# RMSNorm with relu: 4 MB contiguous chunks in place on one hardware DMA queue, and one vector instruction for scale and relu of 8 rows

## The chip, the cores and the metric

The kernel runs on one core of one Trainium2 chip. A time is the device time in microseconds of one execution; "before" is the median of 10 runs. The profile is of one execution. Its span is the time from the first to the last recorded instruction of the core; the execution's own time is a little longer.

## The reference

The input x is f32 of 16 x 1024 x 512, that is 16384 rows of 512 elements (33.55 MB), and the output has the same shape and type. gamma has 512 elements, eps is 1e-5.

```python
rms = np.sqrt(np.mean(x ** 2, axis=-1, keepdims=True) + eps)
x_norm = x / rms * gamma
return np.maximum(x_norm, 0).astype(np.float32)
```

Each row needs the sum of its squares, then every element is multiplied by gamma and by the row's reciprocal root, and is cut at zero. Every byte of x is read once from DRAM and every byte of the output is written once.

## The kernel before

The 128 partitions each own 128 consecutive rows. The loop runs over 16 tiles of K = 8 rows per partition (128 x 4096 elements, 2 MB). Within DRAM a tile is 128 pieces of 16 KB, one per partition, 256 KB apart.

For each tile:

- L62: SP's queue loads `x_tile`. The pool has four buffers of each kind of tile, so at most four loads run ahead; a load into a used buffer waits until ScalarE and VectorE have read the old contents.
- L70: VectorE multiplies x by gamma for all 8 rows in one `tensor_mul` and writes another tile, `xg`. `gammaK` is gamma in SBUF, repeated 8 times by a step of 0 over the rows.
- L74: ScalarE squares each row in one activation, with the row's sum as accumulator output (eight activations, each followed by an accumulator read). The squares themselves go to a scratch tile in SBUF.
- L77: ScalarE takes the root of the 8 means plus eps; L80: VectorE takes the reciprocal, `rstd`.
- L84: VectorE multiplies each row of `xg` by its `rstd` and takes the maximum with 0, one `tensor_scalar` per row, eight per tile. The result `o_tile` is bf16.
- L90: GpSimd's software queue stores `o_tile` and casts it to f32 on the way.

gamma itself is loaded first, by one transfer on SP's queue that reads it 128 times (L48, 256 KB). The loop is written in this order; the order of instructions within an engine is settled by a scheduler at build time (on VectorE the product of a later tile stands between the reciprocal and the scaling of some tiles). Loads and stores are on two queues, which share the 16 DMA engines.

Of the kernel before, what the change touches and what calls it, by code (L numbers as in the profile page):

```python
# [1 line left out]

# [4 lines left out]


@with_exitstack
def kernel(  # L10
    ctx: ExitStack,
    tc: tile.TileContext,
    x: bass.AP,
    gamma: bass.AP,
    eps: bass.AP,
    out: bass.AP,
):
    nc = tc.nc
    P = nc.NUM_PARTITIONS

    x2 = x.flatten_outer_dims()
    out2 = out.flatten_outer_dims()
    n, d = x2.shape
    assert n % P == 0
    rows_per_part = n // P
    inv_d = 1.0 / d

    xv = x2.rearrange("(p r) d -> p r d", p=P)
    ov = out2.rearrange("(p r) d -> p r d", p=P)

    K = 8
    nchunks = rows_per_part // K
    assert rows_per_part % K == 0

    BF = mybir.dt.bfloat16
    F32 = mybir.dt.float32

    singles = ctx.enter_context(tc.tile_pool(name="singles", bufs=1))
    pool = ctx.enter_context(tc.tile_pool(name="pool", bufs=4))
    small = ctx.enter_context(tc.tile_pool(name="small", bufs=4))  # L40

    gamma_sbuf = singles.tile([P, d], F32)
    gamma_bcast = bass.AP(
        tensor=gamma.tensor,
        offset=gamma.offset,
        ap=[[0, P], gamma.ap[0]],
    )
    nc.sync.dma_start(out=gamma_sbuf, in_=gamma_bcast)  # L48

    eps_sbuf = singles.tile([P, 1], F32)  # L50
    nc.vector.memset(eps_sbuf, eps)  # L51

    sq_scratch = singles.tile([P, d], F32)

    gammaK = bass.AP(tensor=gamma_sbuf.tensor, offset=gamma_sbuf[:].offset,
                     ap=[gamma_sbuf[:].ap[0], [0, K], gamma_sbuf[:].ap[1]])

    for i in range(nchunks):
        s = i * K

        x_tile = pool.tile([P, K, d], F32)
        nc.sync.dma_start(out=x_tile, in_=xv[:, s:s + K, :])  # L62

        rstd = small.tile([P, K], F32)
        rms = small.tile([P, K], F32)
        ss = small.tile([P, K], F32)
        xg = pool.tile([P, K, d], F32)
        o_tile = pool.tile([P, K, d], BF)

        nc.vector.tensor_mul(out=xg, in0=x_tile, in1=gammaK)  # L70

        for j in range(K):
            ssj = ss[:, j:j + 1]
            nc.scalar.activation(out=sq_scratch, in_=x_tile[:, j, :],  # L74
                                 func=mybir.ActivationFunctionType.Square,
                                 accum_out=ssj)
        nc.scalar.activation(out=rms, in_=ss,  # L77
                             func=mybir.ActivationFunctionType.Sqrt,
                             bias=eps_sbuf, scale=inv_d)
        nc.vector.reciprocal(out=rstd, in_=rms)  # L80

        for j in range(K):
            rj = rstd[:, j:j + 1]
            nc.vector.tensor_scalar(  # L84
                out=o_tile[:, j, :], in0=xg[:, j, :],
                scalar1=rj, scalar2=0.0,
                op0=mybir.AluOpType.mult, op1=mybir.AluOpType.max,
            )

        nc.gpsimd.dma_start(out=ov[:, s:s + K, :], in_=o_tile)  # L90


# [1 line left out]
_INS = ['x', 'gamma', 'eps']  # L94
_OUTS = [((16, 1024, 512), 'float32')]
#: Inputs that are plain numbers.
_NUMBERS = {'eps': 9.999999747378752e-06}


# [26 lines left out]
```

## Time and profile before

| | |
|---|---|
| median of 10 runs | 165.72 us (165.56 to 165.77) |
| the profiled execution's own time | 165.56 us |
| its span | 163.8 us |
| VectorE (DVE) busy | 122.8 us, 75% of the span |
| ScalarE (ACT) busy | 99.4 us, 61% |
| GpSimd (POOL) busy | 8.9 us, 5% |
| moved by DMA | 67.40 MB, mean 411 GB/s |

Busy time is an instruction's recorded time on its engine. A row of digits is the span in 40 slices, each digit the busy share in tenths. A line of a group gives the source line, engine, operation, output and inputs with partitions x elements and type, the count, then the busy time in us and the mean of one in ns, then the idle time of the engine just before it and what ended most of it. A timeline line gives start and duration in us, engine, line and operation; the bracket gives the idle time before it and what released it. A line of windows gives the window, its length, the busy time of VectorE, ScalarE and GpSimd in it with the number of instructions, the granted TensorE clock, the mean busy share of the DMA engines and the GB/s that they moved. SPq and POOLq are the instruction queues of SP and GpSimd, which issue transfers.

### The profile page before, as it was taken

The page shows a single profiled execution, that of the slowest core. Times are in us where ns is not written, and L with a number is a line of the kernel's source. Part 1 is how long each engine was busy: PE and PEld are TensorE (multiplying, and loading weights), DVE is VectorE, ACT ScalarE, POOL GpSimd, SP SyncE. Part 2 cuts the span into 40 slices and gives each one's busy share as a digit, 9 for nine tenths or more (in the row PEclk, how much of TensorE's full clock was granted, in tenths as well). Part 3 has the DMA queues.
Part 4 walks back from the last instruction along what each step waited for, and adds up shares of the span by engine and source line. Part 5 has one row for each costly group of instructions (what it writes and reads, how often), then busy time and mean ns, then how long its engine had stood idle before and what let it go on. Part 6 is the DMA issues. An engine that isn't in the chain of part 4 may idle for free.

```text
span 163.8 us, 565 instructions
## 1 busy us (share of the span) xinstructions
DVE 122.8 (75%) x161; ACT 99.4 (61%) x274; POOL 8.9 (5%) x20
## 2 busy tenths in 40 slices
DVE  0049979999999999969497794959959497099500
ACT  3049999999993928659193773919559193094000
POOL 0000010001010101010101001010000101001100
DMA  4999999999999999999999999999999999999994
GB/s 118 391 440 428 424 436 384 434 428 424 428 428 424 430 432 420 432 436 416 432 436 416 434 428 416 440 424 428 428 428 440 416 428 440 416 440 380 428 412 192
DMA packets 4755, 67.40 MB, mean 411 GB/s; under 512 B 528, under 2 KB 528, under 8 KB 656
## 3 DMA queue, kind: packets, MB, share of 16 engines
q1 hardware_dynamic: 2448, 33.82, 57.1%
q0 software_dynamic: 2304, 33.56, 49.4%
q14 instruction: 3, 0.02, 0.0%
HBM read 33.82 MB, written 33.55 MB: 411 GB/s over the span
## 4 chain that ended last, share of the span: by engine, by line
issue 50%; DVE 27%; ACT 8%; DMA 6%; POOL 3%; POOLq 0%; SPq 0%
DVE xg L70 15%; DVE o_tile L84 12%; ACT sq_scratch L74 7%; DMA x_tile<-in_x_dram 6%; POOL out_dram L90 3%; ACT L77 1%; DVE rstd L80 1%; ACT rms L77 0%; POOLq L121 0%; SPq L48 0%; POOLq L90 0%
## 5 line engine op out<-in xcount | busy, mean ns | idle before, releaser
L74 ACT ACTIVATE sq_scratch<-x_tile 128x512 f32<-128x512 f32 x128 | 80.6, 629 | 48.6 <-DMA x_tile<-in_x_dram 45.1
L70 DVE TENSOR_TENSOR xg<-x_tile,gamma_sbuf 128x4096 f32<-128x4096 f32 x16 | 70.5, 4407 | 29.1 <-DMA x_tile<-in_x_dram 29.1
L84 DVE TENSOR_SCALAR o_tile<-xg,rstd 128x512 bf16<-128x512 f32 x128 | 52.1, 481 | 0.1
L74 ACT ACTIVATION_READ_ACCUMULATOR sq_scratch<-x_tile 128x1 f32 x128 | 23.9, 186 | 0.0
L90 POOL DMA_DIRECT2D out_dram<-o_tile x16 | 8.7, 541 | 145.7 <-DVE rstd L80 119.6
L77 ACT ACTIVATE rms<-ss,eps_sbuf 128x8 f32<-128x8 f32 x16 | 4.8, 301 | 0.5
L80 DVE RECIPROCAL rstd<-rms 128x8 f32<-128x8 f32 x16 | 3.2, 197 | 1.2 <-ACT rms L77 1.2
L74 ACT ACT_TABLE_LOAD x1 | 1.3, 1283 | 0.7 <-PEq L107 0.7
L77 ACT ACT_TABLE_LOAD x1 | 1.3, 1283 | 0.0
L51 DVE MEMSET eps_sbuf<- 128x1 f32 x1 | 0.1, 59 | 0.8 <-PEq L107 0.8
L107 POOL MEMSET const-float32-0.0<- 128x1 f32 x1 | 0.1, 99 | 0.2 <-issue 0.2
L107 POOL MEMSET const-bfloat16-1.0<- 128x1 bf16 x1 | 0.1, 102 | 0.0
L107 POOL MEMSET const-uint8-127<- 128x1 uint8 x1 | 0.1, 100 | 0.0
L107 POOL MEMSET const-float32-1.0<- 128x1 f32 x1 | 0.1, 99 | 0.0
## 6 DMA issues: line engine op xcount, KB each, us to landing
x_tile<-in_x_dram SPq DMA_DIRECT2D x16, 2048.0 KB, 26.2
out_dram<-o_tile POOLq DMA_DIRECT2D x16, 2048.0 KB, 21.8
gamma_sbuf<-in_gamma_dram SPq DMA_DIRECT2D x1, 256.0 KB, 4.8
```

The lines of the kernel that those rows point to most:

```text
L51: nc.vector.memset(eps_sbuf, eps)
L70: nc.vector.tensor_mul(out=xg, in0=x_tile, in1=gammaK)
L74: nc.scalar.activation(out=sq_scratch, in_=x_tile[:, j, :], func=mybir.ActivationFunctionType.Square, accum_out=ssj)
L77: nc.scalar.activation(out=rms, in_=ss, func=mybir.ActivationFunctionType.Sqrt, bias=eps_sbuf, scale=inv_d)
L80: nc.vector.reciprocal(out=rstd, in_=rms)
L84: nc.vector.tensor_scalar(out=o_tile[:, j, :], in0=xg[:, j, :], scalar1=rj, scalar2=0.0, op0=mybir.AluOpType.mult, op1=mybir.AluOpType.max,)
L90: nc.gpsimd.dma_start(out=ov[:, s:s + K, :], in_=o_tile)
L107: nc = _bacc.Bacc("TRN2", target_bir_lowering=False, num_devices=1)
```

## The change

The rows are cut differently: chunk c of 8 is 2048 consecutive rows, 16 per partition (4 MB), and is one contiguous region of DRAM. There are six slots of 128 x 8192 f32; a chunk is loaded into its slot, worked on in place and stored from it. The output stays f32, so the store casts nothing and goes on SP's queue too. The order of all instructions is now that of the program text: six loads, then S0, S1, L6, S2, L7, S3 to S7 on SP's queue (S and L for the store and the load of a chunk). Within a chunk the work is done in two groups of 8 rows: eight squares (the squares go to a PSUM tile), the root, the gamma product in place, the reciprocal, and one `scalar_tensor_tensor` that takes the maximum with 0 and multiplies by `rstd`, whose access pattern repeats each row's value 512 times with a step of 0. Since `rstd` is positive, maximum and product may change places. gamma is loaded as four rows of 2 KB on ScalarE's queue (into partitions 0, 32, 64 and 96 of a cleared tile) and spread to all partitions by a shuffle on VectorE.

```diff
+    xv = x2.rearrange("(c p k) d -> c p k d", p=P, k=16)
+    ov = out2.rearrange("(c p k) d -> c p k d", p=P, k=16)
-    xv = x2.rearrange("(p r) d -> p r d", p=P)
-    ov = out2.rearrange("(p r) d -> p r d", p=P)
-    K = 8
-    nchunks = rows_per_part // K
+    K = 16
+    G = 8
+    nchunks = rows // K
+    nslots = 6
+    ngroups = K // G
...
+    ctx.enter_context(tc.manual_schedule())
-    nc.sync.dma_start(out=gamma_sbuf, in_=gamma_bcast)
...
+    def load(i):
+        nc.sync.dma_start(out=slot[i % nslots], in_=xv[i])
+    def store(i):
+        nc.sync.dma_start(out=ov[i], in_=slot[i % nslots])
...
+    def compute(i):
+        xt = slot[i % nslots]
+        for g in range(ngroups):
+            a, b = g * G, (g + 1) * G
+            for j in range(a, b):
+                nc.scalar.activation(out=junk, in_=xt[:, j, :], func=ACTF.Square,
+                                     accum_out=ss[i][:, j:j + 1])
+            nc.scalar.activation(out=rms[i][:, a:b], in_=ss[i][:, a:b],
+                                 func=ACTF.Sqrt, bias=eps_sb, scale=inv_d)
+            nc.vector.tensor_mul(out=xt[:, a:b, :], in0=xt[:, a:b, :], in1=gammaG())
+            nc.vector.reciprocal(out=rstd[i][:, a:b], in_=rms[i][:, a:b])
+            r = rstd[i][:, a:b]
+            rb = bass.AP(tensor=r.tensor, offset=r.offset,
+                         ap=[r.ap[0], r.ap[1], [0, d]])
+            nc.vector.scalar_tensor_tensor(
+                out=xt[:, a:b, :], in0=xt[:, a:b, :], scalar=0.0, in1=rb,
+                op0=ALU.max, op1=ALU.mult)
+    nc.vector.memset(gseed, 0.0)
+    nc.vector.memset(eps_sb, eps)
+    for q in range(0, P, 32):
+        nc.scalar.dma_start(out=gseed[q:q + 1, :], in_=gamma[None, :])
+    for i in range(min(nslots, nchunks)):
+        load(i)
+    nc.vector.stream_shuffle(gamma_sb, gseed, [0] * 32)
+    for i in range(min(nslots, nchunks)):
+        compute(i)
+    nxt = nslots
     for i in range(nchunks):
-        x_tile = pool.tile([P, K, d], F32)
-        nc.sync.dma_start(out=x_tile, in_=xv[:, s:s + K, :])
...
-        nc.vector.tensor_mul(out=xg, in0=x_tile, in1=gammaK)
...
-            nc.vector.tensor_scalar(
-                out=o_tile[:, j, :], in0=xg[:, j, :],
-                scalar1=rj, scalar2=0.0,
-                op0=mybir.AluOpType.mult, op1=mybir.AluOpType.max,
-            )
-        nc.gpsimd.dma_start(out=ov[:, s:s + K, :], in_=o_tile)
+        store(i)
+        if i >= 1 and nxt < nchunks:
+            load(nxt)
+            compute(nxt)
+            nxt += 1
```

In the changed kernel's own numbering L59 is the load, L62 the store, L74 the square, L76 the root, L78 the gamma product, L79 the reciprocal, L83 scale and relu, and L94 the shuffle.

More of the change, by code (lines that the diff above doesn't have):

```diff
@@ L6 @@
 from concourse._compat import with_exitstack
+F32 = mybir.dt.float32
+ALU = mybir.AluOpType
+ACTF = mybir.ActivationFunctionType
 @with_exitstack
@@ L23 @@
     n, d = x2.shape
-    assert n % P == 0
-    rows_per_part = n // P
+    rows = n // P
     inv_d = 1.0 / d
-    xv = x2.rearrange("(p r) d -> p r d", p=P)
-    ov = out2.rearrange("(p r) d -> p r d", p=P)
-    K = 8
-    nchunks = rows_per_part // K
-    assert rows_per_part % K == 0
-    BF = mybir.dt.bfloat16
-    F32 = mybir.dt.float32
-    singles = ctx.enter_context(tc.tile_pool(name="singles", bufs=1))
-    pool = ctx.enter_context(tc.tile_pool(name="pool", bufs=4))
-    small = ctx.enter_context(tc.tile_pool(name="small", bufs=4))
@@ L42 @@
[L42 to L46, printed above, removed]
-    )
[L48 to L56, printed above, removed]
@@ L58 @@
-    for i in range(nchunks):
-        s = i * K
-        x_tile = pool.tile([P, K, d], F32)
-        nc.sync.dma_start(out=x_tile, in_=xv[:, s:s + K, :])
[L64 to L84, printed above, removed]
-                out=o_tile[:, j, :], in0=xg[:, j, :],
-                scalar1=rj, scalar2=0.0,
-                op0=mybir.AluOpType.mult, op1=mybir.AluOpType.max,
-            )
-        nc.gpsimd.dma_start(out=ov[:, s:s + K, :], in_=o_tile)
@@ new lines @@
+    xv = x2.rearrange("(c p k) d -> c p k d", p=P, k=16)
[5 more added lines that the diff above has]
+    ngroups = K // G
+    singles = ctx.enter_context(tc.tile_pool(name="singles", bufs=1))
+    slots = ctx.enter_context(tc.tile_pool(name="slots", bufs=1))
+    small = ctx.enter_context(tc.tile_pool(name="small", bufs=1))
+    psum = ctx.enter_context(
+        tc.tile_pool(name="psum", bufs=1, space=bass.MemoryType.PSUM))
@@ new lines @@
+    ctx.enter_context(tc.manual_schedule())
+    gseed = singles.tile([P, d], F32, name="gseed")
+    gamma_sb = singles.tile([P, d], F32, name="gamma_sb")
+    eps_sb = singles.tile([P, 1], F32, name="eps_sb")
+    junk = psum.tile([P, d], F32, name="junk")
+    slot = [slots.tile([P, K, d], F32, name=f"slot{s}") for s in range(nslots)]
+    ss = [small.tile([P, K], F32, name=f"ss{i}") for i in range(nchunks)]
+    rms = [small.tile([P, K], F32, name=f"rms{i}") for i in range(nchunks)]
+    rstd = [small.tile([P, K], F32, name=f"rstd{i}") for i in range(nchunks)]
@@ new lines, in load, with gammaG @@
+    def load(i):
+        nc.sync.dma_start(out=slot[i % nslots], in_=xv[i])
+    def store(i):
+        nc.sync.dma_start(out=ov[i], in_=slot[i % nslots])
+    def gammaG():
+        g = gamma_sb[:]
+        return bass.AP(tensor=g.tensor, offset=g.offset,
+                       ap=[g.ap[0], [0, G], g.ap[1]])
+    def compute(i):
[15 more added lines that the diff above has]
+                op0=ALU.max, op1=ALU.mult)
```

## The prediction

> **What bounds the kernel now.** I read the page's totals first: is any engine full, or is it the transfers?
>
> ```profile
> DVE 122.8 (75%) x161; ACT 99.4 (61%) x274; POOL 8.9 (5%) x20
> DMA  4999999999999999999999999999999999999994
> GB/s 118 391 440 428 424 436 384 434 428 424 428 428 424 430 432 420 432 436 416 432 436 416 434 428 416 440 424 428 428 428 440 416 428 440 416 440 380 428 412 192
> ```
>
> No engine is above 75%, but the DMA row is full from the second slice to the last but one, at about 428 GB/s. So transfers bound it: 67.4 MB / 0.428 = 157.5 us of a 163.8 us span. Next, VectorE in steady state (timeline: start, duration, instruction, idle before) and the stages (window, its length, busy times, clock, DMA share, GB/s):
>
> ```profile
> 100.90 4.43 DVE L70 TENSOR_TENSOR xg<-x_tile,gamma_sbuf 128x4096 f32<-128x4096 f32 x1 [2.09 <-DMA x_tile<-in_x_dram]
> 105.24 3.25 DVE L84 TENSOR_SCALAR o_tile<-xg,rstd 128x512 bf16<-128x512 f32 x8
> 108.41 0.20 DVE L80 RECIPROCAL rstd<-rms 128x8 f32<-128x8 f32 x1
> 110.70 4.43 DVE L70 TENSOR_TENSOR xg<-x_tile,gamma_sbuf 128x4096 f32<-128x4096 f32 x1 [2.10 <-DMA x_tile<-in_x_dram]
> ...
> 10.00:20.00 10.00, 8.97 (x3) 9.12 (x23) 0.00 (x0) 1.00 1.01 433
> 60.00:70.00 10.00, 10.00 (x18) 6.08 (x17) 0.53 (x1) 1.00 1.12 434
> 90.00:100.00 10.00, 7.70 (x10) 6.08 (x17) 0.53 (x1) 1.00 1.11 430
> ```
>
> A tile of 8 rows takes 9.80 us (100.90 to 110.70), in which 2.1 MB come in and 2.1 MB go out; VectorE waits 2.1 us of it for a load. The important row is 60 to 70: there VectorE is busy for the whole 10 us. It is second by only 2 us in 9.8. Then the groups, for prices, and the beginning:
>
> ```profile
> L74 ACT ACTIVATE sq_scratch<-x_tile 128x512 f32<-128x512 f32 x128 | 80.6, 629 | 48.6 <-DMA x_tile<-in_x_dram 45.1
> L70 DVE TENSOR_TENSOR xg<-x_tile,gamma_sbuf 128x4096 f32<-128x4096 f32 x16 | 70.5, 4407 | 29.1 <-DMA x_tile<-in_x_dram 29.1
> L84 DVE TENSOR_SCALAR o_tile<-xg,rstd 128x512 bf16<-128x512 f32 x128 | 52.1, 481 | 0.1
> ```
>
> ```profile
> 0.74 0.36 SPq L48 DMA_DIRECT2D gamma_sbuf<-in_gamma_dram  x1
> 10.57 0.63 ACT L74 ACTIVATE sq_scratch<-x_tile 128x512 f32<-128x512 f32 x1 [8.55 <-DMA x_tile<-in_x_dram]
> 15.46 4.42 DVE L70 TENSOR_TENSOR xg<-x_tile,gamma_sbuf 128x4096 f32<-128x4096 f32 x1 [0.39 <-DMA x_tile<-in_x_dram]
> 16.59 1.28 ACT L77 ACT_TABLE_LOAD   x1
> 20.04 3.26 DVE L84 TENSOR_SCALAR o_tile<-xg,rstd 128x512 bf16<-128x512 f32 x8
> ```
>
> The first tile arrives at 10.57 and the second at 15.46; the gamma product starts at once, beside the squares, because it writes another buffer. Last, the end:
>
> ```profile
> 154.23 0.53 POOL L90 DMA_DIRECT2D out_dram<-o_tile  x1 [2.89 <-DVE o_tile L84]
> ...
> 161.00:161.50 0.50, 0.00 (x0) 0.00 (x0) 0.00 (x0) 1.00 1.04 426
> 161.50:162.00 0.50, 0.00 (x0) 0.00 (x0) 0.00 (x0) 1.00 0.08 0
> ```
>
> Data stops at about 161.5, so 2.3 us lie between the last byte and the end of the span.
>
> [...] the eight scalings take 3.17 us for 4096 elements, the product 4.29 to 4.34, start to start. [...]
>
> **The change, part by part.**
>
> Scale and relu. Removed: per 8 rows, eight tensor_scalar, 3.17 us. Added: one scalar_tensor_tensor over 128x4096 whose second tensor is rstd with step 0. The trace has no such row. [...] I take the product's 4.29, the nearest two-tensor f32 row. It waits for the reciprocal just ahead of it: before, such a start came 0.24 us after the reciprocal's (19.80 to 20.04 in the same timeline), where without a wait it is 0.12. So a group of 8 rows is 4.29 + 0.24 + 4.29 = 8.82, with 0.05 for a start after a wait (4.34 against 4.29) about 8.85 us instead of 7.57. Sixteen groups: 141.6 us. Neither the loads nor ScalarE covers this: VectorE needs 17.7 us for 4 MB in and 4 MB out, and the transfers 2 x 9.8 = 19.6 us, which looks like 2 us to spare per chunk. But VectorE's 141.6 us are not the whole path. They stand between a load and a store which nothing overlaps.
>
> The beginning. In place, the gamma product overwrites x, so it now waits for the eight squares of its group (in the compiled list it waits for ScalarE, where before it waited for transfers alone). The first load is 4.19 MB instead of 2.1. Before, 4.19 MB of x plus 0.26 MB of gamma had landed at about 15.4; gamma leaves SP's queue (four rows of 2 KB on ScalarE's instead), and its stretch ran at only 180 to 190 GB/s. First bytes 1.0 us after issue as before (1.75 against 0.74), 9.8 us of data, 1.8 to 2.5 us [...]: 13.7 to 14.8, I take 14.1. Then eight squares at 0.755 (10.57 to 16.59, with their accumulator reads): 20.2. Squares write PSUM instead of SBUF; I keep 0.755 [...]. The table load (1.28) and the root (0.30) are hidden by the product: rms is there at 21.8, the reciprocal wants it at 24.5. The second group's squares end at 27.9, before VectorE's 29.05: only 1.2 us of cover; later groups gain, since ScalarE needs 6.3 us a group and VectorE 8.85.
>
> The end. VectorE finishes at 20.2 + 141.6 = 161.8. Only then can the last 4.19 MB store start (before, the last store was 2.1 MB and 16 groups of VectorE had finished at 153.9): 0.1 us to SP, 1.0 to the first byte, 9.8 of data, 2.3 to the end: 13.2. Span 175.0.
>
> One queue in a fixed order. Loads L0 to L5 fill it until 1.8 + 6 x 9.8 = 60.6. Stores S0 and S1 are ready at 37.9 and 55.6 and run behind them to 80.2; L6 (issued when S0 has landed, about 72) runs to 90.0, S2 (ready 73.3) to 99.8, L7 to 109.6. SP stands still at each store's wait for VectorE, and behind it the next load, so what is late next would be the squares of chunk 6 or 7. Chunk 6 is wanted by VectorE at 20.2 + 12 x 8.85 = 126.4 and its first squares can end at 98; chunk 7 is wanted at 144.1, first squares 117.4. Some 27 us of cover: zero. S3 to S5 run to 139.0; S6 is ready at 144.1, so the queue is then idle, waiting for VectorE. Without the cover a late load adds its lateness one for one.
>
> Everything else: clearing the gamma seed, four small loads and a shuffle are done before 14.1 by any price near the rows shown (gamma landed 4.8 us after issue), and gamma is wanted at 20.2. ScalarE's four issues lie in its wait for L0. GpSimd's sixteen issues of 0.53 go; they were hidden by the transfers. The bytes are the same but for the gamma broadcast.
>
> Sum against the profiled execution: span 175.0, plus the 1.76 us outside it (165.56 - 163.8) is 176.8; the median stands 0.16 above that execution: 176.9, or 6.8% slower.
>
> **Rivals.**
>
> (a) [...] VectorE gets under the transfers, and these set the end: 1.8 + 67.1 / 0.428 + 2.3 = 160.9, time 162.8: faster. From when on: 20.2 + 16p + 13.2 is under 163.8 for p under 8.15, so the new instruction must take less than 3.6 us. For it: the scaling before had this rate. Against: that had one tensor, this has two.
>
> (b) The step-0 operand or the two operations halve the rate: group 13.15, span 20.2 + 210.4 + 13.2 = 243.8, time 245.7. For it: no row shows the form. [...]
>
> (c) Transfers in one direction on one queue are slower, say 350 GB/s (12.0 us a chunk): the first load and the last store add 2.2 each, and L7 lands at about 134, its squares at 142, still ahead of 144.1: 181.3. Against: loads alone ran at 433 (10 to 20 us), and 426 at the end were stores alone, though from bf16.
>
> **How the numbers follow.** VectorE as the bound at the price taken: 0.83, own range 174 to 180 (start 0.8 either way, group 8.8 to 9.05, tail 12.5 to 15). (a) 0.06, (b) 0.05, (c) 0.06. The range with 8 in 10 is 173.5 to 182.0, with (c) in it and the two prices (a) and (b) out. The ten runs shown lie within 0.13% of each other, so about 0.2% can be told from no change: faster 0.06, same 0.01, slower 0.93.
>
> **What would show it.** VectorE at 10 of 10 us in every window from 20 to 160; L83 as 128x4096 at 4.3 to 4.4 us x16; first L78 6 us after the first square; DMA below full after about 140, and 13 us between VectorE's end and the span's. It would be wrong if L83 were below 3.6 us, or VectorE had waits for ScalarE or loads after 30 us.

## The result and the profile after

| | before | after |
|---|---|---|
| median | 165.69 us (29 runs, 165.56 to 165.84) | 175.75 us (8 runs, 175.59 to 175.91) |
| the profiled execution's own time | 165.56 us | 175.85 us |
| its span | 163.8 us | 174.1 us |
| VectorE busy | 122.8 us | 143.3 us |
| ScalarE busy | 99.4 us | 98.5 us |
| moved by DMA | 67.40 MB | 67.14 MB |

The ratio is 1.0607, 95% interval 1.0598 to 1.0617. The kernel is 6% slower; 176.9 was forecast.

The page after, its totals and the row of transfers:

```profile
DVE 143.3 (82%) x52; ACT 98.5 (57%) x274; POOL 0.2 (0%) x4
DVE  1001599999999999999999999999999999999200
DMA  7999999999999999999999999999999808940885
```

Before, the DMA row was full to the end; now it has holes in the last fifth, with two slices of 0 and one of 4, while VectorE's row is 9 from the sixth slice until VectorE is through. The two have changed places. The groups show by which instructions:

```profile
L78 DVE TENSOR_TENSOR slot<-slot,gamma_sb 128x4096 f32<-128x4096 f32 x16 | 70.7, 4419 | 4.1 <-ACT junk L74 4.1
L83 DVE SCALAR_TENSOR_TENSOR slot<-slot,rstd 128x4096 f32<-128x4096 f32 x16 | 70.8, 4425 | 0.5
```

The new L83 has the price of the product, to 6 ns. 70.8 us stand where 52.1 stood. In all of the span VectorE waits only once for ScalarE, 4.1 us, and for a load only through gamma at the start. Now the timelines (start, duration, instruction, idle before): ScalarE's first square, then VectorE's first group and its last:

```profile
13.25 0.60 ACT L74 ACTIVATE junk<-slot 128x512 f32<-128x512 f32 x1 [9.14 <-DMA slot<-in_x_dram]
...
14.49 0.72 DVE L94 STREAM_SHUFFLE gamma_sb<-gseed 128x512 f32<-128x512 f32 x1
19.28 4.42 DVE L78 TENSOR_TENSOR slot<-slot,gamma_sb 128x4096 f32<-128x4096 f32 x1 [4.06 <-ACT junk L74]
23.62 0.20 DVE L79 RECIPROCAL rstd<-rms 128x8 f32<-128x8 f32 x1
23.85 4.42 DVE L83 SCALAR_TENSOR_TENSOR slot<-slot,rstd 128x4096 f32<-128x4096 f32 x1
28.19 4.42 DVE L78 TENSOR_TENSOR slot<-slot,gamma_sb 128x4096 f32<-128x4096 f32 x1
...
152.91 4.42 DVE L78 TENSOR_TENSOR slot<-slot,gamma_sb 128x4096 f32<-128x4096 f32 x1
157.24 0.20 DVE L79 RECIPROCAL rstd<-rms 128x8 f32<-128x8 f32 x1
157.47 4.43 DVE L83 SCALAR_TENSOR_TENSOR slot<-slot,rstd 128x4096 f32<-128x4096 f32 x1
```

From 19.28 to 152.91 are 15 groups of 8.91 us without a gap. VectorE ends at 161.9, and only then is the last store issued. The windows around it:

```profile
140.00:150.00 10.00, 9.97 (x4) 0.00 (x0) 0.00 (x0) 1.00 0.62 263
150.00:160.00 10.00, 9.97 (x4) 0.00 (x0) 0.00 (x0) 1.00 0.37 157
...
163.00:172.00 9.00, 0.00 (x0) 0.00 (x0) 0.00 (x0) 1.00 0.95 408
```

Between 140 and 160 the transfers run at 263 and 157 GB/s, where the same queue moved 423 between 20 and 30: it has nothing to send, because every chunk behind is still with VectorE. Between 163 and 172 only the last store moves. So the time is now a chain of three parts: 19.3 us until VectorE can begin, 142.6 us of VectorE, 12.2 us for the last store.

### The profile page after: what moved, and what is told of

It is laid out like the page before. It is cut to its first block, busy times and chain, and to the rows that moved or that the text cites. A ratio compares the mean times of both kernels' runs of the same rounds, so it can differ in the third digit from the quotient of the medians.

```text
span 174.1 us, 415 instructions
## 1 busy us (share of the span) xinstructions
DVE 143.3 (82%) x52; ACT 98.5 (57%) x274; POOL 0.2 (0%) x4
## 2 busy tenths in 40 slices
DMA packets 2315, 67.14 MB, mean 386 GB/s; under 512 B 260, under 2 KB 260, under 8 KB 264
## 4 chain that ended last, share of the span: by engine, by line
DVE 49%; ACT 23%; issue 14%; DMA 7%
DVE slot L78 30%; ACT junk L74 21%; DVE slot L83 18%; DMA slot<-in_x_dram 7%; ACT rms L76 1%; DVE rstd L79 1%; ACT L76 1%
## 5 line engine op out<-in xcount | busy, mean ns | idle before, releaser
L74 ACT ACTIVATE junk<-slot 128x512 f32<-128x512 f32 x128 | 76.8, 600 | 22.5 <-DMA slot<-in_x_dram 19.0
L78 DVE TENSOR_TENSOR slot<-slot,gamma_sb 128x4096 f32<-128x4096 f32 x16 | 70.7, 4419 | 4.1 <-ACT junk L74 4.1
L83 DVE SCALAR_TENSOR_TENSOR slot<-slot,rstd 128x4096 f32<-128x4096 f32 x16 | 70.8, 4425 | 0.5
L74 ACT ACTIVATION_READ_ACCUMULATOR junk<-slot 128x1 f32 x128 | 23.9, 186 | 0.0
L94 DVE LOAD_MASK_SELECT gamma_sb<-gseed x1 | 0.0, 14 | 13.1 <-DMA gseed<-in_gamma_dram 13.1
L76 ACT ACTIVATE rms<-ss,eps_sb 128x8 f32<-128x8 f32 x16 | 4.8, 301 | 0.5
L79 DVE RECIPROCAL rstd<-rms 128x8 f32<-128x8 f32 x16 | 3.1, 196 | 0.0
L87 DVE MEMSET gseed<- 128x512 f32 x1 | 0.5, 485 | 0.9 <-PEq L120 0.9
L94 DVE STREAM_SHUFFLE gamma_sb<-gseed 128x512 f32<-128x512 f32 x1 | 0.7, 724 | 0.0
```

Of the source, the lines that this page charges most:

```text
L74: nc.scalar.activation(out=junk, in_=xt[:, j, :], func=ACTF.Square, accum_out=ss[i][:, j:j + 1])
L76: nc.scalar.activation(out=rms[i][:, a:b], in_=ss[i][:, a:b], func=ACTF.Sqrt, bias=eps_sb, scale=inv_d)
L78: nc.vector.tensor_mul(out=xt[:, a:b, :], in0=xt[:, a:b, :], in1=gammaG())
L79: nc.vector.reciprocal(out=rstd[i][:, a:b], in_=rms[i][:, a:b])
L83: nc.vector.scalar_tensor_tensor(out=xt[:, a:b, :], in0=xt[:, a:b, :], scalar=0.0, in1=rb, op0=ALU.max, op1=ALU.mult)
L87: nc.vector.memset(gseed, 0.0)
```

## Experiments

The theory under test (A): VectorE's path sets the end, with one load and one store at its ends that nothing overlaps. The rivals differ from run to run and stand with each. Ratios are against runs of the kernel before on the same chip.

### Eight scalings again

```diff
-            nc.vector.scalar_tensor_tensor(
-                out=xt[:, a:b, :], in0=xt[:, a:b, :], scalar=0.0, in1=rb,
-                op0=ALU.max, op1=ALU.mult)
+            for j in range(a, b):
+                nc.vector.tensor_scalar(
+                    out=xt[:, j, :], in0=xt[:, j, :],
+                    scalar1=rstd[i][:, j:j + 1], scalar2=0.0,
+                    op0=ALU.mult, op1=ALU.max)
```

> The changed kernel with scale and relu as eight tensor_scalar per group again (in place, f32 out); all else as changed. Theory A (VectorE's rate, between a load and a store that nothing overlaps, sets the end): a group costs 4.34 + 0.23 + 3.17 = 7.75 us, VectorE's path is 19.3 + 16 x 7.75 + 12.2 = 155.5, so the transfers bound it: 1.8 + 67.1 MB at 428 GB/s + 2.3 = 160.9, time 162 to 163.5. Theory B (one queue in a fixed order costs the time, the vector instruction does not): 170 or more.

Measured 164.37 us, ratio 0.9926 (0.9908 to 0.9944): 11.4 us less than with the single instruction, and 0.7% below the time before. Its VectorE timeline and, from its windows, the end:

```profile
119.91 4.42 DVE L78 TENSOR_TENSOR slot<-slot,gamma_sb 128x4096 f32<-128x4096 f32 x1
124.24 0.20 DVE L79 RECIPROCAL rstd<-rms 128x8 f32<-128x8 f32 x1
124.47 3.26 DVE L81 TENSOR_SCALAR slot<-slot,rstd 128x512 f32<-128x512 f32 x8
127.65 4.42 DVE L78 TENSOR_TENSOR slot<-slot,gamma_sb 128x4096 f32<-128x4096 f32 x1
...
150.00:155.00 5.00, 0.00 (x0) 0.00 (x0) 0.00 (x0) 1.00 1.02 439
158.00:160.00 2.00, 0.00 (x0) 0.00 (x0) 0.00 (x0) 1.00 0.12 49
```

A group takes 7.74 us (119.91 to 127.65), VectorE is through at 143.2, and the transfers go on at 439 GB/s without it. Theory B falls: the queue, its order, the large chunks and working in place are all still there. Without the single instruction the whole loss is gone, and more; that it does harm only together with the rest of the change is shown by the runs below. But the time is 0.9 us above the upper end of what A expected; that gap is taken up below.

### Half of the chunks

The single instruction in chunks 0 to 3, eight scalings in chunks 4 to 7 (`if i < 4` around the two forms).

> The changed kernel with the single vector instruction in chunks 0 to 3 and eight tensor_scalar per group in chunks 4 to 7. Theory A (VectorE's path): 19.28 + 8 x 8.91 + 8 x 7.74 + 12.2 = 164.7 span, time 166.4; it stands above the 162.1 at which the run with eight tensor_scalar everywhere ended. If the gain per group were not added up one for one, it would lie at the middle of the two, 170.

Measured 166.43 us, ratio 1.0046 (1.0033 to 1.0059), as expected. VectorE ends at 152.4 (149.14 + 3.26), and 12.2 us follow to the end of the span (164.6), as in the change. Eight groups fewer with the single instruction save 9.3 us against the change: each of them costs its 1.17 us once VectorE's path stands above the transfers.

### The first load and the last store in halves

```diff
-        nc.sync.dma_start(out=slot[i % nslots], in_=xv[i])
+        parts = 2 if i == 0 else 1
+        w = K // parts
+        for h in range(parts):
+            nc.sync.dma_start(out=slot[i % nslots][:, h * w:(h + 1) * w, :],
+                              in_=xv[i][:, h * w:(h + 1) * w, :])
```

The store has the same form, with `parts = 2 if i == nchunks - 1`.

> The changed kernel with the first load and the last store issued as two transfers of 2 MB each, one per group of 8 rows; the vector instructions stay. Theory A: the first square starts 4.9 us earlier and the last store has half the data after VectorE's end, 4.9 us each: 166 us, up to 167 if gamma (spread at 15.2 in the changed kernel) becomes what the first product waits for. Theory B2 (only VectorE's busy time counts, the ends are hidden): 175.8.

Measured 165.84 us, ratio 1.0012 (1.0005 to 1.0018). Nearly ten microseconds are gone with the same 143.3 us of VectorE. The lines are of its VectorE timeline:

```profile
9.99 0.72 DVE L102 STREAM_SHUFFLE gamma_sb<-gseed 128x512 f32<-128x512 f32 x1
14.12 4.42 DVE L86 TENSOR_TENSOR slot<-slot,gamma_sb 128x4096 f32<-128x4096 f32 x1 [3.41 <-ACT junk L82]
...
152.32 4.42 DVE L91 SCALAR_TENSOR_TENSOR slot<-slot,rstd 128x4096 f32<-128x4096 f32 x1
```

The first product comes 5.2 us earlier (14.12 against 19.28), the last instruction ends at 156.7, and the span of 164.0 leaves 7.3 us after it instead of 12.2. Both ends are shown to lie on the path, with 5.2 and 4.9 us, where 4.9 us for the 2 MB of each was expected. Gamma came earlier too (see the last section).

### The products of the first chunk not in place

```diff
-            nc.vector.tensor_mul(out=xt[:, a:b, :], in0=xt[:, a:b, :], in1=gammaG())
+            src = slot[5] if i == 0 else xt
+            nc.vector.tensor_mul(out=src[:, a:b, :], in0=xt[:, a:b, :], in1=gammaG())
```

L83 reads `src`, and L5 is issued after the first chunk's arithmetic.

> The changed kernel, with the gamma products of the first chunk (two groups) written into the sixth slot, which is still empty, instead of in place; L5 is issued after them. Theory A: the first product starts when gamma is spread (15.2) instead of at 19.28, the first scaling when the first roots are there (20.9, plus the reciprocal: 21.1 instead of 23.85): 2.7 us less, 173.0. Theory D (the wait that working in place adds is hidden): 175.8.

Measured 173.01 us, ratio 1.0449 (1.0432 to 1.0467): 2.7 us less than the change. Its VectorE timeline:

```profile
14.99 4.43 DVE L79 TENSOR_TENSOR slot<-slot,gamma_sb 128x4096 f32<-128x4096 f32 x1
20.65 0.20 DVE L80 RECIPROCAL rstd<-rms 128x8 f32<-128x8 f32 x1 [1.24 <-ACT rms L76]
20.89 4.42 DVE L84 SCALAR_TENSOR_TENSOR slot<-slot,rstd 128x4096 f32<-128x4096 f32 x1
```

The wait for the squares is gone from the product, and a shorter one stands before the reciprocal. L5 is issued only after 34 us here, but no wait for a load appears: the first scaling starts 2.96 us earlier than in the change (20.89 against 23.85), and the span is shorter by 3.0 (171.1 against 174.1). Theory D falls: working in place costs what it adds to the wait of the first group. Behind that group VectorE had no waits in the change either, so there it costs no time.

### Both of these

> The changed kernel with the first load and the last store in two transfers of 2 MB, and the gamma products of the first chunk written to the empty sixth slot; the single vector instruction stays in all groups. Theory A: 2.75 us less than the split alone (span 164.0), 161.3, unless the transfers end later: the run with eight tensor_scalar, whose transfers were never held up, ended at 162.1. Time 163.0 to 164.4, faster than before. If the two savings overlap: 165.8.

Measured 164.47 us, ratio 0.9923 (0.9908 to 0.9938), slightly above the range and 0.8% below the time before, with the single instruction in every group. VectorE ends at 154.1 here (149.65 + 4.42) and the span at 162.9, 8.8 us later instead of 7.3: the transfers, at 423 to 427 GB/s from 130 to 150, are now up against it.

### Stores on the other queue

```diff
-        nc.sync.dma_start(out=ov[i], in_=slot[i % nslots])
+        nc.gpsimd.dma_start(out=ov[i], in_=slot[i % nslots])
```

> The changed kernel with its stores on GpSimd's software queue instead of SP's, same order of issue. Theory A: VectorE never waits for a load after the first, so nothing moves: 175.4 to 176.3 (up to 0.5 for a slower issue of the last store). Theory B (the single queue): at least 2 us faster.

Measured 176.55 us, ratio 1.0659 (1.0643 to 1.0675), 0.8 us slower than the change, a little outside A's range. VectorE ends at 161.6 there, so the difference is after it: 13.0 us to the end of the span (174.6) instead of 12.2. The issue of the last store begins 0.30 us after VectorE's end on GpSimd (161.92) and is recorded at 0.53 us; on SP it was 0.03 and 0.33 us (161.93). The single queue costs nothing in this kernel; for the last store it is the quicker one.

### The instruction in the kernel before

```diff
-        for j in range(K):
-            rj = rstd[:, j:j + 1]
-            nc.vector.tensor_scalar(
-                out=o_tile[:, j, :], in0=xg[:, j, :],
...
+        nc.vector.scalar_tensor_tensor(
+            out=o_tile, in0=xg, scalar=0.0, in1=rb,
+            op0=mybir.AluOpType.max, op1=mybir.AluOpType.mult)
```

> The kernel before, with the eight tensor_scalar of a tile replaced by the one scalar_tensor_tensor (bf16 out); tiles of 2 MB, queues and buffers as before. Theory A: a tile costs VectorE 4.29 + 4.29 + 0.12 = 8.70 us, which is under the 9.80 us of its transfers; first tile at 10.6, last VectorE instruction no earlier than 33.2 + 14 x 8.7 = 155.0, store of 2 MB after it about 9: 164 span, time 165.7 to 167.5. Theory E (the instruction by itself makes the kernel slower, wherever it stands): 16 x 1.12 = 18 us more, or a good part of it, over 170.

Measured 166.55 us, ratio 1.0053 (1.0040 to 1.0066). The groups of that kernel, and the end of its VectorE timeline:

```profile
L85 DVE SCALAR_TENSOR_TENSOR o_tile<-xg,rstd 128x4096 bf16<-128x4096 f32 x16 | 70.7, 4420 | 0.1
L70 DVE TENSOR_TENSOR xg<-x_tile,gamma_sbuf 128x4096 f32<-128x4096 f32 x16 | 70.2, 4387 | 14.8 <-DMA x_tile<-in_x_dram 14.8
...
151.90 4.42 DVE L85 SCALAR_TENSOR_TENSOR o_tile<-xg,rstd 128x4096 bf16<-128x4096 f32 x1
```

Some eighteen microseconds more of VectorE cost 0.8 us here (166.55 against 165.74 before on the same chip), since VectorE gives up waits for loads instead (29.1 us before, 14.8 now): its last instruction ends at 156.3 instead of 153.9. Theory E falls: the instruction is no loss as such. It becomes one where VectorE begins at 19.3 and a store of 12.2 us must follow.

### What holds the run with eight scalings above its transfers

That run was expected at 162 to 163.5 and took 164.37. The first run below leaves out all arithmetic and stores x; the second does the same and also loads the four gamma rows on ScalarE's queue; the third has the arithmetic with eight scalings and loads gamma on SP's queue between L0 and L1.

> The changed kernel without any arithmetic: the same loads and stores in the same order on the same queue, a store waiting for its load; the output is x. If the run with eight tensor_scalar (164.4) was bound by its transfers alone, this takes as long, 164 to 164.6. If something else held it above the 162.6 worked out from 428 GB/s, this takes 162.6.

> The transfers alone, as in the run without arithmetic (162.7), and beside them the four gamma rows on ScalarE's queue; no arithmetic, the output is x. Theory F: about 164. Theory G: 162.7, within the spread of that run (162.2 to 163.3).

> The run with eight tensor_scalar per group, with the four gamma rows loaded on SP's queue between L0 and L1 instead of on ScalarE's. Theory F (the second queue puts some DMA engines behind, and these end last): 1 to 1.5 us faster than with gamma on ScalarE's queue (164.4), about 163. Theory G (it is the arithmetic beside the transfers, or SP's waits for it): 164.4.

| | median us | lowest to highest |
|---|---|---|
| transfers alone | 162.72 | 162.21 to 163.33 |
| transfers and gamma | 161.87 | 161.79 to 163.15 |
| eight scalings, gamma on SP's queue | 164.61 | 163.57 to 164.94 |
| eight scalings, gamma on ScalarE's queue | 164.37 | 164.11 to 164.78 |

The transfers alone take the 162.6 that were worked out from 428 GB/s. Gamma on a second queue does not make them slower, and moving it does not help: theory F falls. With arithmetic beside them the same transfers take 1.7 to 2.7 us longer, judging by the medians; the kernel before took 165.63 to 165.74 on the three chips of these runs. The traces do not show where. The run with eight scalings moves only 49 GB/s from 158 to 160, but the transfers alone end in the same way (the line has no VectorE or ScalarE, which do nothing there):

```profile
158.00:160.00 2.00, 0.00 (x0) 1.00 0.08 33
```

The four profiled executions have spans of 161.4 to 162.1, so they lie too close together to tell the two kinds apart. Only about 0.3 us of the difference can be placed: in the two runs with eight scalings, 2.0 to 2.2 us of an execution's time lie outside its span, in the two without arithmetic 1.8. Which part of the arithmetic or of SP's waits costs the rest was not tried and stays open. The change itself doesn't depend on it, since its queue is idle at the end.

## Why the prediction was right

The mechanism, its place and the size were right: VectorE's path sets the end, the new instruction has the price taken for it, and the start and the end of the path came out within a microsecond each. That VectorE's end agrees to 0.1 us is luck, since a start forecast 0.9 us too late and groups forecast 1.0 us too short in sum cancel there. The sum against the trace:

| step of the prediction | forecast | measured |
|---|---|---|
| first load seen by ScalarE | 14.1 | 13.25 |
| first product starts | 20.2 | 19.28 |
| a group of 8 rows | 8.85 | 8.91 |
| VectorE ends | 161.8 | 161.9 |
| from there to the end of the span | 13.2 | 12.2 |
| span | 175.0 | 174.1 |
| outside the span | 1.76 | 1.75 |

- **Scale and relu.** The price taken, an estimate from the nearest two-tensor row, the product's, was right: L83 takes 4.34 us to the next L78, and its record is 4425 ns with f32 output and 4420 with bf16. That the second tensor has step 0 and that there are two operations costs nothing over the product (4419 ns), whose gamma is repeated by a step of 0 too; no run has a product without one. Whether it is the second tensor that keeps the instruction from the pace of the scalings, or its form, no run separates. Rival (a) needed less than 3.6 us and rival (b) more than 8; both are out. The eight scalings are 1.37 times as fast as the product (3.17 against 4.34). The group was 0.06 too low: in place, both long instructions take 4.34 us from start to start, and I gave only one of the two the extra 0.05. The product takes it even where it had not waited (28.19 to 32.53); why is not shown. Over 16 groups that is 1 us.
- **The beginning.** L0 landed 0.85 us earlier than taken, even below the range given for it (13.7 to 14.8). That range was added up wrongly: its own terms, 1.75 + 9.8 + (1.8 to 2.5), give 13.35 to 14.05. The measured 13.25 lies only 0.1 below that. The 1.8 to 2.5 us were an estimate: before, gamma and the first tile are 2.36 MB, 2.35 MB had been moved in all by 8.75 us (at a mean of 268 GB/s), and the first square came at 10.57, 1.8 us later. What fills that time is not shown. The squares kept their 0.75 us each; in PSUM an activation is recorded at 600 ns instead of 629, but the next one starts no sooner (13.25 to 14.00). The wait that working in place adds was on the path, as the run without it shows. The second group's cover, forecast at 1.2 us, was about 1.4: its product never waited.
- **The end.** One microsecond less than the sum of its parts; which of them was shorter is not shown. The halved store confirmed the part that is data (4.9 us for 2 MB).
- **One queue.** VectorE waited for no load after the first (ScalarE did, 2.6 us for L6 and 7.2 us for L7, inside the cover), and stores on another queue changed 0.8 us, the wrong way. Rival (c) is out: loads alone ran at 423 GB/s between 20 and 30, and the last store alone at 408.
- **Gamma** was placed too early. I had it spread before 14.1; it was spread at 15.2. The 4.1 us left until 19.28 hid it, so it cost nothing.
- **Rival (a)'s size.** Its mechanism occurred in the run with eight scalings, where a group falls below 8.15 us. Its figure, 162.8, is met by the transfers alone and missed by 1.6 us with arithmetic beside them.

## What to carry to other kernels

Compare an engine with the transfers not by its time per tile alone, but by first load + all its work + last store: here 17.8 us per chunk of VectorE against 19.6 of transfers looked safe and lost, because 31.5 us of load, squares and store stood around it. Make the first load and the last store small: with all other transfers left at 4 MB, halving just these two took the time from 175.75 to 165.84 us, nearly all of the loss. Joining eight instructions into one was no gain here: the single form took 4.34 us where the eight took 3.17.

## What the runs showed of the hardware beyond that

- Four rows of 2 KB on ScalarE's queue, issued from 1.43 to 2.8 us, were only seen by VectorE at 14.47, just behind the 4 MB that SP's queue had begun to load at 0.73 (first square 13.25). With a first load of 2 MB (first square 8.10) they were there at 9.96. So in these runs the small transfers on the second queue did not pass the large one that was under way; why is not shown.
- With the squares in PSUM instead of SBUF the recorded activation is 29 ns shorter (600 against 629), between these two kernels, and the pace of activations with an accumulator read is the same (0.75 us). The destination was not changed alone.
- 67.1 MB of loads and stores in fixed order on one hardware queue took 161.9 to 162.7 us as whole kernels; with VectorE and ScalarE at work beside them, 164.4 to 164.6.
